# Half of the expert down-projection by three passes of high and low parts, and the shift of x in rows of 512 over three engines

## The chip, the core and the metric

One core of a Trainium2 chip runs the whole program. The metric is the device time of one execution in microseconds (us). The kernel before takes 1606.7 us (median of three runs, 1605.95 to 1608.96).

## The reference, cut to what matters

A decoder layer on 1024 tokens of width 2048, all in float32: a mixing sub-layer (spatial gating and stick-breaking attention), then a mixture of experts. Each token picks two of 32 experts. What an expert does with the rows `xb` of its tokens:

```python
def expert_block(args):
    xb, e = args
    act = jax.nn.silu(xb @ w_gate[e]) * (xb @ w_up[e])
    return act @ w_down[e]
```

`w_gate[e]` and `w_up[e]` are 2048 x 256, `w_down[e]` is 256 x 2048. The rows `xb` are normalised, scaled and shifted by a per-column vector (`* (1 + scale2) + shift2`) before the experts; the results are weighted, gated and added into the output.

## The kernel before, in words

The change lies in the last stage, which runs the 32 experts one after the other from about 945 us on. For every expert one tile of 128 token rows is gathered into `xg` (`gather_e`, L1327, issued by GpSimd, POOL), scaled, turned by TensorE (PE) in four chunks of 512 columns (`turn`, L1257), shifted, multiplied with gate and up weights (`gateup`, L1285), passed through SiLU (`act`, L1294), turned again (`turn_act`, L1300), multiplied with the down weights in four column groups of 512 (`down`, L1307), and scattered with addition into the output (`scatter_e`, L1330, POOL).

Precision is kept in two ways. Gate and up run in three passes of a faster matmul format (`float32r`): a weight tile is rounded to a high part `wh` by ScalarE (ACT, L1281), VectorE (DVE) subtracts it to get the low part `wl` (L1282), and `gateup` adds xh*wh, xh*wl and xl*wh. The shift makes `xh` and `xl` from PSUM, in four ACT and four DVE instructions of 128 columns each per chunk (L1270, L1272). The down product is one plain float32 matmul per half of the 256 rows (L1314), which the chip runs as two instructions; so a column group is four PE instructions.

The order of work is written by hand (L1398 to L1436), and every engine runs its instructions in the order in which the program issues them. The loop over experts e has eight steps q = 0 to 7. Step q multiplies two of the 16 chunks of weights (six matmuls), prepares weights three steps ahead, and interleaves what belongs to the neighbours: in the odd steps chunk q//2 of the next expert is turned ahead of `gateup` and shifted at the end of the step; the previous expert's `turn_act` comes at q = 2 and its four `down` groups at q = 3, 4, 5, 6; after the last of them, at q = 6, its scatter is issued. The gather for expert e+2 is issued at the head of loop e. Weights come in tiles of 1 MB (four for gate and up, two for down) through a ring of 12 slots, issued by SyncE (SP) in the program's order as slots come free.

Gather and scatter go in up to three pieces of rows (`pieces`, L1317). The second and third are inside `tc.If` on the expert's token count, on POOL alone: where a piece is not needed, POOL's sequencer runs instead an instruction that advances the semaphore (`INC_SWDGE_SEM`, shown at L1322).

Of the kernel before, what the change touches and what calls it, by code (L numbers as in the profile page):

```python
# [10 lines left out]
F32 = mybir.dt.float32  # L11
F32R = mybir.dt.float32r
I32 = mybir.dt.int32
AF = mybir.ActivationFunctionType
ALU = mybir.AluOpType
AX = mybir.AxisListType

P = 128
S = 1024
D = 2048  # L20
# [6 lines left out]
NE = 32  # L27
# [31 lines left out]
def body(ctx, tc, A, out):  # L59
    nc = tc.nc  # L60
    V, G, T, SC, SY = nc.vector, nc.gpsimd, nc.tensor, nc.scalar, nc.sync
    PS = bass.MemoryType.PSUM

    keep = ctx.enter_context(tc.tile_pool(name="keep", bufs=1))
# [2 lines left out]
    moe = ctx.enter_context(tc.tile_pool(name="moe", bufs=1))  # L67
    big_ = ExitStack()
    big = big_.enter_context(tc.tile_pool(name="big", bufs=2, reuse_waits="tile"))
    c1 = ExitStack()  # L70
    c1k = c1.enter_context(tc.tile_pool(name="c1k", bufs=1, reuse_waits="tile"))

# [7 lines left out]
    hcol = keep.tile([P, 10], F32, name="hcol")  # L80
    bgr = keep.tile([P, 36], F32, name="bgr")
    mhalf = keep.tile([P, 4], F32, name="mhalf")
    ident_r = keep.tile([P, P], F32R, name="ident_r")
    negm_r = keep.tile([P, P], F32R, name="negm_r")
    tri_r = keep.tile([P, P], F32R, name="tri_r")
    comp_r = keep.tile([P, P], F32R, name="comp_r")
    ccol = c1k.tile([P, 16], F32, name="ccol")
    tcst = []
    gcol = c1k.tile([P, 2, 16], F32, name="gcol")
# [356 lines left out]
    with tc.manual_schedule():  # L446
# [114 lines left out]
        for t in range(HT):  # L561
            b = (30, 33, 34, 35)[t]
# [488 lines left out]
            self.R = onehot(rt, 0, self.t)  # L1051

    def onehot(pool, b, t):
        R = []
        for i in range(2):
            R.append(pool.tile([P, P], F32, name="R", bufs=4 if b else 2))
            V.tensor_scalar(R[i], iota, float(b * P), rank[i][:, t:t + 1], op0=ALU.add, op1=ALU.is_equal)
        return R

# [133 lines left out]
    def pool(name, bufs=1):  # L1193
        return ctx.enter_context(tc.tile_pool(name=name, bufs=bufs, reuse_waits="tile"))
# [3 lines left out]
    ypools = [pool("ypool")]  # L1198
    wpa = pool("wpa", 4)
    wpb = pool("wpb", 4)  # L1200
    xpool = pool("xpool", 6)
    wpe = pool("wpe")
    wpr = pool("wpr")
    lpool = pool("lpool", 4)
    mw = pool("mw", 3)
    sl = pool("sl")
    xg = [pool("xg0").tile([P, D], F32, name="xg0")]
    wpc = pool("wpc", 2)
    hpool = pool("hpool", 4)
    xg.append(pool("xg1").tile([P, D], F32, name="xg1"))  # L1210
    wpools = [wpa] * 4 + [wpc] * 2 + [wpr] + [wpb] * 4 + [wpe]
    nw = [0]

    def wtile(shape):
        nw[0] += 1
        return wpools[(nw[0] - 1) % len(wpools)].tile(shape, F32, name="wx")
# [11 lines left out]
    class Expert:  # L1228
# [13 lines left out]

        def load_out(self):
            self.wd = []
            for f in range(2):
                w = wtile([P, D])
                SY.dma_start(w, self.wd_[f * P:(f + 1) * P, :])
                self.wd.append(w)

        def scale(self, b, on_act=True):  # L1250
# [13 lines left out]
                c = b * 4 + j  # L1264
                T.transpose(self.p[:, j, :], self.x[:, c * P:(c + 1) * P], ident)  # L1265

        def shift(self, b):
            xh, xl = self.xh[b], self.xl[b]
            for j in range(4):
                SC.activation(xh[:, j, :], self.p[:, j, :], AF.Identity, bias=b2c[:, b * 4 + j:b * 4 + j + 1])  # L1270
            for j in range(4):
                V.scalar_tensor_tensor(xl[:, j, :], self.p[:, j, :], b2c[:, b * 4 + j:b * 4 + j + 1],  # L1272
                                       xh[:, j, :].bitcast(F32), op0=ALU.add, op1=ALU.subtract)
# [26 lines left out]
        def turn_act(self):  # L1300
            p = pt2.tile([P, 4, P], F32, name="tp")
            for f in range(2):
                T.transpose(p[:, f, :], self.a[:, f * P:(f + 1) * P], ident)
            self.aT = mw.tile([P, 2, P], F32, name="actT")
            SC.activation(self.aT, p[:, 0:2, :], AF.Copy)  # L1305

        def down(self, cg):  # L1307
            if cg == 0:
                ypools.append(ypools.pop(0))
                self.y = ypools[0].tile([P, D], F32, name="y2")  # L1310
            cs = slice(cg * 512, (cg + 1) * 512)
            d = pd2.tile([P, 512], F32, name="dn")
            for f in range(2):
                T.matmul(d, self.aT[:, f, :], self.wd[f][:, cs], start=(f == 0), stop=(f == 1))  # L1314
            V.tensor_tensor(self.y[:, cs], d, gate2[:, cs], op=ALU.mult)  # L1315

    def pieces(e, move):  # L1317
# [12 lines left out]
    def scatter_e(e, y):  # L1330
        pieces(order[e], lambda r, ix: scatter(y[r], ix))

    cregs = {}
    if True:
# [56 lines left out]
            ex[0].scale(b, b % 2 == 0)  # L1391
        for b in range(3):
            ex[0].turn(b)
            ex[0].shift(b)
        V.tensor_scalar(mx[:, 1:8], iota[0:1, FIRST + 1:FIRST + 8], float(P), mx[:, 0:1], op0=ALU.mult, op1=ALU.is_lt)
        V.tensor_reduce(mx[:, 0:1], mx[:, 1:8], axis=AX.X, op=ALU.add)
        V.tensor_copy(nblk, mx[:, 0:1])
        for e in range(NE):  # L1398
            x, nx, px = ex[e], ex[e + 1] if e + 1 < NE else None, ex[e - 1] if e else None
            if nx and e:  # L1400
                nx.load_in()
            if e:
                x.load_out()
            if 0 < e < NE - 2:
                begin(e + 2)
            at_q = (2, 3, 4, 5, 6) if nx else (3, 5, 6, 7, 8)
            for q in range(8):
                if nx and q % 2 and (e, q) != (0, 1):
                    nx.turn(q // 2)
                x.gateup(q)  # L1410
                if e == 0 and q == 1:
                    x.turn(3)
                    x.shift(3)
                    begin(2)
                    nx.scale(0)
                if px and q == at_q[0]:
                    px.turn_act()
                if px and q in at_q[1:]:
                    px.down(at_q.index(q) - 1)
                    if q == at_q[4]:  # L1420
                        scatter_e(e - 1, px.y)
                if q < 5:
                    x.split(q + 3)
                elif nx:
                    nx.split(q - 5)
                if q % 2 == 0:
                    if q < 6 and nx:
                        nx.scale(q // 2 + 1)
                    elif q == 6 and e + 2 < NE:
                        ex[e + 2].scale(0)  # L1430
                if q == 7:
                    x.act()
                if (e, q) == (0, 1):
                    nx.turn(0)
                if nx and q % 2:
                    nx.shift(q // 2)  # L1436
        px.down(3)
        scatter_e(NE - 2, px.y)
        x.turn_act()
        for cg in range(4):  # L1440
            x.down(cg)
        scatter_e(NE - 1, x.y)

    ms.close()
# [4 lines left out]
    with tc.If(nmore > 0):  # L1449
        val = wtile([P, NT, 2, 3, NE])  # L1450
        for t in range(NT):
            for i in range(2):
                E, c = sl.tile([P, NE], F32, name="E", bufs=2), slice(t, t + 1)
                V.tensor_scalar(E, iom, ex_col[i][:, c], None, op0=ALU.is_equal)
                for a, f in enumerate((tok[:, c], wt_col[:, t, i:i + 1], rs_col[:, c])):
                    V.tensor_scalar(val[:, t, i, a, :], E, f, None, op0=ALU.mult)
        for b in range(1, NT):
            pt_ = pd2.tile([P, 512], F32, name="dn")
            table_start(pt_)
            for t in range(NT):  # L1460
                place(pt_, onehot(sl, b, t), [val[:, t, i] for i in range(2)], t == NT - 1)
            tb = sl.tile([P, NE, 3], I32, name="tb")
            V.tensor_copy(tb[:, :, 0], pt_[:, 0:NE])
            for i in (1, 2):
                V.tensor_copy(tb[:, :, i].bitcast(F32), pt_[:, i * NE:(i + 1) * NE])
            G.dma_start(tab_d[(b - 1) * NE:b * NE].rearrange("e p w -> p e w"), tb)
        with tc.For_i(0, nmore, 1) as b:
            with tc.For_i(0, NE, 1) as e:
                tb = mw.tile([P, 3], I32, name="tb2", bufs=2)
                SY.dma_start(tb, tab_d[ds(b * NE + e, 1)].rearrange("o p w -> (o p) w"))  # L1470
                V.memset(xg[0], 0.0)
                x = Expert(A["w_gu"][ds(e, 1)].rearrange("o q p k g f -> (o q) p k g f"),
                           A["w_down"][ds(e, 1)].rearrange("o d f -> (o d) f"),
                           xg[0], tb[:, 1:2].bitcast(F32), tb[:, 2:3].bitcast(F32))
                x.load()
                gather(xg[0], tb[:, 0:1])
                for c in range(4):
                    x.scale(c)
                    x.turn(c)
                    x.shift(c)  # L1480
                for q in range(8):
                    x.split(q)
                    x.gateup(q)
                x.act()
                x.turn_act()
                for c in range(4):
                    x.down(c)
                scatter(x.y, tb[:, 0:1])

# [33 lines left out]
```

## Time and profile before

| | |
|---|---|
| median of three runs | 1606.7 us |
| the profiled execution | 1609.03 us |
| its span, first to last instruction | 1607.2 us |
| mean granted clock of PE | 0.976 |
| instructions | 21345 |

The span is what the views below cut up. Times in the views are microseconds from its start, unless they are marked ns or stand as the mean of one instruction, which is in ns. "Busy" is time in which an engine executes; PE is the matmuls, PEld the loading of PE's weights ahead of them. In a timeline row the first number is the start, the second the duration, and a bracket gives the idle time of that engine before it and what the profile names as the releaser. The profile lists matmuls with overlapping ends, so the pace of PE is read from starts.

### The profile page before, as it was taken

Reading aid. Unit: us, or ns where it says so; the run is one execution under the profiler, and the core shown is the slowest. Engines: PE = TensorE matmul, PEld = TensorE weight load, DVE = VectorE, ACT = ScalarE, POOL = GpSimd, SP = SyncE. Lnnn points to the kernel's source line nnn. Section 1 sums busy time; section 2 is a strip of 40 time slices with the busy share of each in tenths; the row PEclk is TensorE's granted clock in tenths of the full one; section 3 lists DMA queues with packets and bytes.
Section 4 is the critical chain, followed back from the end, with each engine's and each line's share of the span. In section 5 each row is a group of like instructions: output and inputs, shape, how many; then the busy total and the mean of one; then the engine's idle time right before and its main releaser. Section 6 shows DMA issues by size and latency. Waiting matters only on the chain.

```text
span 1607.2 us, 21345 instructions
## 1 busy us (share of the span) xinstructions
PE 1516.0 (94%) x6818; PEld 1150.1 (72%) x6818; DVE 1216.5 (76%) x2220; ACT 949.0 (59%) x2016; POOL 309.7 (19%) x286
## 2 busy tenths in 40 slices
PE   4999998999999888899999969999999999999996
PEld 4788886788888665578878856666666666666663
DVE  5889675867787588768865768888888888888783
ACT  4442587754435577532222468777777777777771
POOL 2000132010011244310001211223222112223121
PEclk8899999999999999999999969999999999999998
DMA  9987477778876000368866648999999999999992
GB/s 378 353 317 245 153 258 287 238 246 298 301 272 228 9 1 1 114 225 281 295 211 264 234 167 317 364 362 374 362 383 359 355 361 361 350 375 345 377 331 43
DMA packets 94393, 433.94 MB, mean 270 GB/s; under 512 B 13072, under 2 KB 13184, under 8 KB 64192
## 3 DMA queue, kind: packets, MB, share of 16 engines
q1 hardware_dynamic: 82000, 377.54, 63.3%
q0 software_dynamic: 11984, 52.85, 11.3%
q10 hardware_dynamic: 288, 2.10, 0.3%
q8 instruction: 56, 0.92, 0.2%
q14 instruction: 65, 0.53, 0.1%
HBM read 399.89 MB, written 43.02 MB: 276 GB/s over the span
## 4 chain that ended last, share of the span: by engine, by line
PE 69%; DMA 12%; DVE 5%; ACT 5%; issue 5%; POOL 2%; SPq 0%; POOLq 0%; ACTq 0%; DVEq 0%; another core or an unknown queue 0%
PE acc L322 22%; PE gu L1291 16%; PE dn L1314 10%; PE acc L867 9%; DMA out<-y,idx 4%; DMA xg<-u_d,idx 3%; PE tp L1265 3%; DMA wm<-in_w_mod 2%; DMA out<-xi 2%; PE lg L913 1%; PE yp L719 1%; POOL sl L683 1%; PE z L655 1%; DVE macc L182 1%; DVE sp L681 1%
## 5 line engine op out<-in xcount | busy, mean ns | idle before, releaser
L1282 DVE TENSOR_TENSOR wl<-wx,wh 128x1024 fp32r<-128x1024 f32 x256 | 309.3, 1218 | 14.7 <-ACT wh L1281 13.7
L1281 ACT ACTIVATE wh<-wx 128x1024 fp32r<-128x1024 f32 x256 | 273.5, 1070 | 34.0 <-PE gu L1291 33.5
L1314 PE MATMUL dn<-wx,actT 128*128 128x512 f32 x512 | 240.1, 592 | 0.6 <-ACT actT L1305 0.5
L1291 PE MATMUL gu<-wh,xh 128*128 128x512 f32 x512 | 239.0, 467 | 0.0
L182 DVE SCALAR_TENSOR_TENSOR macc<-wm,sc_c,macc 128x512 f32<-128x512 f32 x296 | 222.2, 751 | 12.0 <-DMA wm<-in_w_mod 3.9
L322 PE MATMUL acc<-wh,hh 128*128 128x512 f32 x640 | 209.6, 398 | 3.8 <-ACT hh L278 1.8
L322 PE MATMUL acc<-wl,hh 128*128 128x512 f32 x640 | 206.6, 393 | 2.8 <-DVE wl L307 2.6
L322 PE MATMUL acc<-wh,hl 128*128 128x512 f32 x640 | 205.4, 391 | 0.3 <-DVE hl L279 0.3
L1291 PE MATMUL gu<-wl,xh 128*128 128x512 f32 x512 | 202.6, 396 | 0.1
L1291 PE MATMUL gu<-wh,xl 128*128 128x512 f32 x512 | 201.6, 394 | 0.0
L1224 POOL DMA_INDIRECT out<-y,idx x52 | 94.4, 1816 | 438.9 <-DVE y L1315 432.8
L867 PE MATMUL acc<-wo,yh 128*128 128x512 f32 x512 | 170.2, 414 | 0.0
L1315 DVE TENSOR_TENSOR y<-dn,gate 128x512 f32<-128x512 f32 x128 | 88.5, 691 | 103.2 <-PE dn L1314 103.2
L1270 ACT ACTIVATE xh<-tp,b2c 128x128 fp32r<-128x128 f32 x512 | 146.9, 383 | 19.8 <-PE tp L1265 19.8
L1314 PEld LDWEIGHTS dn<-wx,actT 128*128 128x128 f32 x512 | 96.1, 188 | 75.4 <-issue 63.2
L1272 DVE SCALAR_TENSOR_TENSOR xl<-tp,b2c,xh 128x128 fp32r<-128x128 f32 x512 | 143.4, 343 | 4.1 <-ACT xh L1270 4.1
L322 PEld LDWEIGHTS acc<-wl,hh 128*128 128x128 f32 x640 | 120.8, 189 | 29.9 <-DVE wl L307 5.0
L322 PEld LDWEIGHTS acc<-wh,hl 128*128 128x128 f32 x640 | 120.7, 189 | 26.6 <-DVE hl L279 1.0
L322 PEld LDWEIGHTS acc<-wh,hh 128*128 128x128 f32 x640 | 119.2, 189 | 27.9 <-ACT hh L278 1.9
L307 DVE TENSOR_TENSOR wl<-w,wh 128x1024 fp32r<-128x1024 f32 x80 | 97.5, 1220 | 33.5 <-ACT wh L306 33.4
L306 ACT ACTIVATE wh<-w 128x1024 fp32r<-128x1024 f32 x80 | 83.0, 1053 | 64.2 <-PE acc L322 54.2
L1291 PEld LDWEIGHTS gu<-wl,xh 128*128 128x128 f32 x512 | 97.2, 190 | 30.3 <-issue 14.8
(246 smaller groups left out, 2316.3 us busy)
## 6 DMA issues: line engine op xcount, KB each, us to landing
wx<-in_w_gu SPq DMA_DIRECT2D x128, 1024.0 KB, 22.5
wm<-in_w_mod SPq DMA_DIRECT2D x160, 512.0 KB, 5.3
wx<-in_w_down SPq DMA_DIRECT2D x64, 1024.0 KB, 21.6
w<-in_w_in SPq DMA_DIRECT2D x80, 512.0 KB, 5.4
x<-in_w_mod SPq DMA_DIRECT2D x16, 1024.0 KB, 6.1
wo<-in_w_out SPq DMA_DIRECT2D x16, 512.0 KB, 4.8
xi<-in_x SPq DMA_DIRECT2D x24, 256.0 KB, 5.9
out<-xi SPq DMA_DIRECT2D x24, 256.0 KB, 3.9
```

The costliest lines, as they stand in the source:

```text
L182: V.scalar_tensor_tensor(self.acc, t[:, j, :], sc, self.acc, op0=ALU.mult, op1=ALU.add)
L307: V.tensor_tensor(wl, w, wh.bitcast(F32), op=ALU.subtract)
L322: T.matmul(accs[t], a, b, start=(first and j == 0 and n == 0), stop=(last and j == 1 and n == 2))
L867: T.matmul(acc, y[a][:, c, ts_], w[b][:, c % 2, :], start=(n_ == 0 and i == 0), stop=(n_ == 7 and i == 2))
L1224: return G.indirect_dma_start(out=out, out_offset=bass.IndirectOffsetOnAxis(ap=idx, axis=0), in_=y, in_offset=None, bounds_check=S - 1, oo ...
L1270: SC.activation(xh[:, j, :], self.p[:, j, :], AF.Identity, bias=b2c[:, b * 4 + j:b * 4 + j + 1])
L1272: V.scalar_tensor_tensor(xl[:, j, :], self.p[:, j, :], b2c[:, b * 4 + j:b * 4 + j + 1], xh[:, j, :].bitcast(F32), op0=ALU.add, op1=ALU.sub ...
L1281: SC.activation(self.wh[q], w, AF.Copy)
L1282: low = lambda: V.tensor_tensor(self.wl[q], w, self.wh[q].bitcast(F32), op=ALU.subtract)
L1291: T.matmul(self.gu, a[c // 4][:, c % 4, :], b[q][:, k, :], start=(c == 0 and i == 0), stop=(c == 15 and i == 2))
L1314: T.matmul(d, self.aT[:, f, :], self.wd[f][:, cs], start=(f == 0), stop=(f == 1))
L1315: V.tensor_tensor(self.y[:, cs], d, gate2[:, cs], op=ALU.mult)
```

## The change

Two of the four column groups of `down` (1 and 3) are computed as three `float32r` passes. ACT rounds the group's weights to `dh`, DVE makes the low part `dl` (`split_down`), and `turn_act` makes `ah` (ACT) and `al` (POOL) beside `actT`. The down weights are stored and loaded in two halves of columns instead of two halves of rows, so that a half is free once its two groups are done. `shift` becomes one DVE addition over 512 columns from PSUM into a new single-buffered tile `xf`; its rounding (ACT) and subtraction (POOL) are returned as a function, which the loop calls in the following step (`later`). The first expert's chunks keep the old form. Buffers shrink or move to make room: `xpool` 6 to 5, `mw` 3 to 1, four constants to a pool that is closed before the experts.

```diff
     def onehot(pool, b, t):
-        R = []
+        if b:
+            both = pool.tile([P, 4, P], F32, name="xf")
+            R = [both[:, i, :] for i in range(2)]
+        else:
+            R = [pool.tile([P, P], F32, name="R", bufs=2) for _ in range(2)]
...
-    xpool = pool("xpool", 6)
+    xpool = pool("xpool", 5)
...
-    mw = pool("mw", 3)
+    mw = pool("mw")
     sl = pool("sl")
...
+    dpool = pool("dpool")
...
         def load_out(self):
             self.wd = []
-            for f in range(2):
-                w = wtile([P, D])
-                SY.dma_start(w, self.wd_[f * P:(f + 1) * P, :])
+            for h in range(2):
+                w = wtile([P, 2, D // 2])
+                SY.dma_start(w, self.wd_[h])
                 self.wd.append(w)
...
-        def shift(self, b):
+        def shift(self, b, fast=False):
             xh, xl = self.xh[b], self.xl[b]
+            if not fast:
+                x = sl.tile([P, 4, P], F32, name="xf")
+                V.tensor_tensor(x, self.p, b2c[:, b * 4:b * 4 + 4].unsqueeze(2).to_broadcast([P, 4, P]), op=ALU.add)
+
+
+                def parts():
+                    SC.activation(xh, x, AF.Copy)
+                    G.tensor_tensor(xl, x, xh.bitcast(F32), op=ALU.subtract)
+                return parts
...
             SC.activation(self.aT, p[:, 0:2, :], AF.Copy)
+            self.ah = mw.tile([P, 2, P], F32R, name="actH")
+            self.al = mw.tile([P, 2, P], F32R, name="actL")
+            SC.activation(self.ah, p[:, 0:2, :], AF.Copy)
+            G.tensor_tensor(self.al, self.aT, self.ah.bitcast(F32), op=ALU.subtract)
+
+        def wd_of(self, cg):
+            return self.wd[cg // 2][:, :, cg % 2 * 512:cg % 2 * 512 + 512]
+
+        def split_down(self, cg):
+            self.dh = dpool.tile([P, 2, 512], F32R, name="dh")
+            self.dl = dpool.tile([P, 2, 512], F32R, name="dl")
+            SC.activation(self.dh, self.wd_of(cg), AF.Copy)
+            V.tensor_tensor(self.dl, self.wd_of(cg), self.dh.bitcast(F32), op=ALU.subtract)
...
-            for f in range(2):
-                T.matmul(d, self.aT[:, f, :], self.wd[f][:, cs], start=(f == 0), stop=(f == 1))
+            if cg % 2:
+                for f in range(2):
+                    for i, (a, b) in enumerate(((self.ah, self.dh), (self.ah, self.dl), (self.al, self.dh))):
+                        T.matmul(d, a[:, f, :], b[:, f, :], start=(f == 0 and i == 0), stop=(f == 1 and i == 2))
+            else:
+                for f in range(2):
+                    T.matmul(d, self.aT[:, f, :], self.wd_of(cg)[:, f, :], start=(f == 0), stop=(f == 1))
             V.tensor_tensor(self.y[:, cs], d, gate2[:, cs], op=ALU.mult)
...
+        later = []
         for e in range(NE):
...
                 if px and q == at_q[0]:
                     px.turn_act()
+                    px.split_down(1)
                 if px and q in at_q[1:]:
                     px.down(at_q.index(q) - 1)
+                    if q == at_q[2]:
+                        px.split_down(3)
                     if q == at_q[4]:
                         scatter_e(e - 1, px.y)
...
+                if later:
+                    later.pop()()
                 if nx and q % 2:
-                    nx.shift(q // 2)
+                    later.append(nx.shift(q // 2))
         px.down(3)
         scatter_e(NE - 2, px.y)
+        x.split_down(1)
         x.turn_act()
         for cg in range(4):
             x.down(cg)
+            if cg == 1:
+                x.split_down(3)
```

## Rows read from the trace of the kernel before

**Rows 1.** The page, part 1: busy time, share and instructions of each engine.

```profile
PE 1516.0 (94%) x6818; PEld 1150.1 (72%) x6818; DVE 1216.5 (76%) x2220; ACT 949.0 (59%) x2016; POOL 309.7 (19%) x286
```

**Rows 2.** Busy time by stage; columns: stretch, us, busy time of each engine, PEclk, DMA, GB/s.

```profile
1100.00:1200.00 100.00, 99.92 (x410) 68.70 (x409) 82.81 (x145) 75.07 (x150) 27.05 (x17) 1.00 1.00 372
...
1200.00:1220.00 20.00, 20.00 (x83) 13.82 (x82) 16.57 (x29) 15.17 (x31) 3.17 (x2) 1.00 0.97 379
```

**Rows 3.** The chain of waits from 900 us on: start, us, work.

```profile
1199.48 1.72 PE dn L1314 x4
1201.20 1.39 PE gu L1291 x6
...
1219.48 1.72 PE dn L1314 x4
```

**Rows 4.** Costliest groups of instructions, and those of POOL: busy us, mean ns.

```profile
L1282 DVE TENSOR_TENSOR wl<-wx,wh 128x1024 fp32r<-128x1024 f32 x256 | 309.3, 1218 | 14.7 <-ACT wh L1281 13.7
L1281 ACT ACTIVATE wh<-wx 128x1024 fp32r<-128x1024 f32 x256 | 273.5, 1070 | 34.0 <-PE gu L1291 33.5
...
L1270 ACT ACTIVATE xh<-tp,b2c 128x128 fp32r<-128x128 f32 x512 | 146.9, 383 | 19.8 <-PE tp L1265 19.8
L1272 DVE SCALAR_TENSOR_TENSOR xl<-tp,b2c,xh 128x128 fp32r<-128x128 f32 x512 | 143.4, 343 | 4.1 <-ACT xh L1270 4.1
...
L849 DVE TENSOR_TENSOR yld<-tr,hcol 128x512 f32<-128x512 f32 x4 | 2.7, 684 | 0.0
L853 ACT ACTIVATE yh<-yld 128x512 fp32r<-128x512 f32 x4 | 2.5, 634 | 2.4 <-DVE yld L849 2.4
...
L683 POOL TENSOR_TENSOR sl<-sp,sh 128x512 fp32r<-128x512 f32 x24 | 30.7, 1279 | 41.1 <-DVE sh L682 30.8 <-PE yp L719 8.0 <-PE cum L697 2.3
L854 POOL TENSOR_TENSOR yl<-yld,yh 128x512 fp32r<-128x512 f32 x8 | 11.7, 1463 | 44.4 <-ACT yh L853 44.4
...
L683 POOL TENSOR_TENSOR sl<-sp,sh 128x256 fp32r<-128x256 f32 x8 | 5.8, 731 | 8.7 <-DVE sh L682 6.0 <-PE cum L709 2.3 <-PE yp L719 0.3
```

**Rows 5.** Timeline of DVE around the end of one expert.

```profile
1204.34 0.69 DVE L1315 TENSOR_TENSOR y<-dn,gate 128x512 f32<-128x512 f32 x1 [0.24 <-PE dn L1314]
...
1207.62 1.12 DVE L1272 SCALAR_TENSOR_TENSOR xl<-tp,b2c,xh 128x128 fp32r<-128x128 f32 x4
1208.67 1.21 DVE L1282 TENSOR_TENSOR wl<-wx,wh 128x1024 fp32r<-128x1024 f32 x1
```

**Rows 6.** Timeline of PE's weight loads: gateup of step 3, then the second down group.

```profile
1211.29 0.19 PEld L1291 LDWEIGHTS gu<-wl,xh 128*128 128x128 f32 x1
...
1215.56 0.41 PEld L1314 LDWEIGHTS dn<-wx,actT 128*128 128x128 f32 x2
```

**Rows 7.** Timeline of POOL: scatters (L1224) and the gathers (L1220) behind them.

```profile
1187.74 1.31 POOL L1224 DMA_INDIRECT out<-y,idx  x1 [0.30 <-issue]
...
1205.31 2.12 POOL L1224 DMA_INDIRECT out<-y,idx  x1 [14.57 <-DVE y L1315]
1211.16 1.05 POOL L1220 DMA_INDIRECT xg<-u_d,idx  x1 [3.73 <-ACT xh L1270]
...
1469.40 1.68 POOL L1224 DMA_INDIRECT out<-y,idx  x1 [0.30 <-issue]
```

**Rows 8.** All scatters; POOL's skips (L1322) before and after 1330 us, min/median/max ns.

```profile
L1224 POOL DMA_INDIRECT out<-y,idx x52 | 94.4, 1816 | 438.9 <-DVE y L1315 432.8
...
L1322 POOLq INC_SWDGE_SEM  x50: 1475/2302/2682, 953.3 to 1327.2; - x50
...
L1322 POOLq INC_SWDGE_SEM  x36: 377/712/1097, 1332.4 to 1596.5; - x36
```

**Rows 9.** Busy time by stage around two waits of PE; columns as in rows 2.

```profile
826.00:830.00 4.00, 1.24 (x9) 0.94 (x8) 2.84 (x5) 1.10 (x4) 0.00 (x0) 1.00 0.34 131
830.00:834.00 4.00, 4.00 (x14) 3.09 (x13) 1.23 (x1) 0.83 (x1) 0.00 (x0) 0.58 0.25 43
...
1487.00:1492.00 5.00, 4.04 (x20) 2.77 (x19) 2.57 (x6) 4.27 (x9) 2.76 (x3) 1.00 1.05 385
```

More of the change, by code (lines that the diff above doesn't have):

```diff
@@ L69, in body @@
     big = big_.enter_context(tc.tile_pool(name="big", bufs=2, reuse_waits="tile"))
+    big1 = big_.enter_context(tc.tile_pool(name="big1", bufs=1))
+    ident_r, negm_r, tri_r, comp_r = (big1.tile([P, P], F32R, name=f"cr{i}") for i in range(4))
     c1 = ExitStack()
@@ L82, in body @@
     mhalf = keep.tile([P, 4], F32, name="mhalf")
[L83 to L86, printed above, removed]
     ccol = c1k.tile([P, 16], F32, name="ccol")
@@ L1053, in onehot @@
     def onehot(pool, b, t):
-        R = []
+        if b:
[3 more added lines that the diff above has]
+            R = [pool.tile([P, P], F32, name="R", bufs=2) for _ in range(2)]
         for i in range(2):
-            R.append(pool.tile([P, P], F32, name="R", bufs=4 if b else 2))
             V.tensor_scalar(R[i], iota, float(b * P), rank[i][:, t:t + 1], op0=ALU.add, op1=ALU.is_equal)
@@ L1393, in body @@
             ex[0].turn(b)
-            ex[0].shift(b)
+            ex[0].shift(b, True)
         V.tensor_scalar(mx[:, 1:8], iota[0:1, FIRST + 1:FIRST + 8], float(P), mx[:, 0:1], op0=ALU.mult, op1=ALU.is_lt)
@@ L1412, in body @@
                     x.turn(3)
-                    x.shift(3)
+                    x.shift(3, True)
                     begin(2)
@@ L1472, in body @@
                 x = Expert(A["w_gu"][ds(e, 1)].rearrange("o q p k g f -> (o q) p k g f"),
-                           A["w_down"][ds(e, 1)].rearrange("o d f -> (o d) f"),
+                           A["w_down"][ds(e, 1)].rearrange("o h p k f -> (o h) p k f"),
                            xg[0], tb[:, 1:2].bitcast(F32), tb[:, 2:3].bitcast(F32))
@@ L1479, in body @@
                     x.turn(c)
-                    x.shift(c)
+                    x.shift(c)()
                 for q in range(8):
@@ L1486, in body @@
                 for c in range(4):
+                    if c % 2:
+                        x.split_down(c)
                     x.down(c)
@@ L1500 @@
     arr = {"x": I["x"][0], "w_mod": tiles(I["w_mod"], 2), "w_in": tiles(I["w_in"][0], 2),
-           "w_out": tiles(I["w_out"][0], 2), "w_gu": wgu, "w_down": I["w_down"][0]}
+           "w_out": tiles(I["w_out"][0], 2), "w_gu": wgu,
+           "w_down": I["w_down"][0].reshape(NE, 2, P, 2, D // 2).transpose(0, 3, 2, 1, 4)}
     arr["consts"] = const_blob()
```

## The prediction, made before the changed kernel was run

> **What bounds the kernel now.** I read the page first: PE is busy for 94% of the span, far ahead of DVE and ACT [rows 1]. An average says nothing of a stage, so the busy time by stage comes next. In the experts, the only stage that the change touches, PE is busy for all of 100 us, DVE for 83%, ACT for 75%; in one period of 20 us DVE works 16.57, ACT 15.17 and POOL only 3.17 us [rows 2]. The chain of waits shows the beat: the same down group starts at 1199.48 and at 1219.48, so an expert takes 20.0 us, and PE hardly waits in it [rows 3]. PE's instruction stream is the bound, the DMA engines are full beside it (share 0.97 to 1.00) [rows 2], and POOL looks idle. The views to read last are therefore the timelines, for what the change makes PE wait for.
>
> **The change part by part.** *PE.* Four float32 down instructions hold PE for 1.72 us, six float32r instructions for 1.39 [rows 3]. The new groups 1 and 3 are six of the latter: 0.33 us saved each, 0.66 an expert. For 31 experts that is 20.5 us. The last expert has nothing beside its downs; there `dh` and `dl` for group 3 can only be made after group 1 (one buffer), about 1.07 + 1.21 us [rows 4, 5] against one group of 1.72, which eats its 0.66: nothing.
>
> *DVE.* Per expert it loses four groups of shift instructions, 1.12 each [rows 5], and gains four additions over 512 columns from PSUM, 0.68 each, and two `dl`, 1.22 each [rows 4]: 16.57 - 4.48 + 2.74 + 2.44 = 17.27 us [rows 2]. Against a period of 19.34 that fits, with little to spare.
>
> *ACT.* Out go four groups of four, 146.9/128 = 1.15 us each; in come four roundings of 0.63, two `dh` of 1.07 and `ah` (no row has it in this form; half of a 512-column rounding is 0.32, the whole 0.63, I take 0.4, nearer the half) [rows 4]: 15.17 - 4.60 + 2.54 + 2.14 + 0.4 = 15.65 us. `dh` of group 3 waits for PE to end group 1 and holds the weight rounding behind it; those roundings are made three steps ahead, so I cost it at nothing; without that lead each would cost up to a step, 2.5 us.
>
> *POOL.* It gains `al`, 0.73, and four subtractions over 512 columns, 1.28 each, or 1.46 by the slower row [rows 4]. In sum that is 6 us on an engine that is busy for 3. The order matters, not the sum. The tile `xf` has one buffer: DVE can't write the next chunk until POOL has subtracted the one before. The subtraction of chunk 2 is issued at step 6, *behind the scatter*, and that of chunk 3 at step 0, *behind the gather*. POOL takes its instructions in order, and DVE does too, with the low parts of gateup's weights behind its addition.
>
> **First wait: chunk 2 behind the scatter.** Count from the start of the last `y`, 1204.34 [rows 5]. The scatter starts at 0.97 and takes 2.12 [rows 7]. Gateup of step 3 loads for its `wl` at 1211.29 [rows 6], 6.95 after `y`. DVE needs 0.69 for `xf` and 1.21 for that `wl` before it, so the subtraction must be over 5.05 after `y`. By pieces of the scatter:
> - Two pieces: the second runs at 3.09 + 0.30 to 4.70 [rows 7], the subtraction from 5.0 to 6.3: 1.25 us late.
> - Three: the third adds 0.30 + 1.68 [rows 7], 8.3: 3.2 us late.
> - One: the two skipped pieces hold POOL's sequencer. They have a median of 2.30 us each in the first two thirds of the stage, 0.71 in the last third [rows 8]. The trace of before shows this as the gather starting 3.73 us after the scatter's end with nothing else for it to wait for [rows 7]. Early, the subtraction goes from 0.92 + 2 x 2.30 + 0.25 = 5.8 to 7.1: 2.0 late. Late in the stage it goes from 3.4 to 4.7: in time.
>
> The 52 scatter instructions [rows 8] are, counted in that timeline, 16 experts of one piece, 12 of two and 4 of three. Of those of one piece 14 come in loops with a later chunk to shift, 8 before 1330 us. Sum: 12 x 1.25 + 4 x 3.2 + 8 x 2.0 = 44 us. PE recovers none of it, since the next `y` comes later by the same time.
>
> **Second wait: chunk 3 behind the gather.** The new `dl` of group 1 stands on DVE behind `xf` of the next chunk 0, which waits for the subtraction of chunk 3. The group starts at 1215.56 [rows 6]; its second pass, one instruction (0.23) later, needs `dl`, 11.45 after `y`. Early in the stage, with one piece each: gather and two more skips follow the first subtraction's issue by 1.5 us and take 2 x 2.3 + 0.2, so chunk 3 is subtracted from 12.1 to 13.4, `xf` and `dl` end at 15.3: 3.9 late in all, 1.9 more than the first wait. By the same steps, with each pair's own pieces and skips, four pairs of one piece give 8.3 more, four with a gather of three pieces 8.6, the rest 4.6: 21.5 us. Its lower bound is nothing, if the first wait has set PE back far enough.
>
> **The sum.** 44 + 21.5 - 20.5 = 45 us slower. The profiled execution took 1609.03 us, 2.3 above the median; 1654 on its scale is 1652 on that of the median.
>
> **Edits at nothing.** The two loads of down weights have the same count and size; the first half's slot comes free two groups earlier. With `xpool` at 5 a chunk's buffer is that of the chunk before it in the current expert, whose gateup ended two steps earlier. With `mw` at 1, `act` and `actT` are read out steps before they are written again. The moved constants and the second form of `onehot` run no instruction in this stage. If one of these covers were gone, a wait of a step, 2.5 us an expert, would appear at `xh` or `actT`.
>
> **The rivals.**
> - *Faster: POOL keeps up.* Decided by the subtraction of chunk 2: if it ends within 5.05 us of `y` in nearly all experts, PE gains 20.5. For it: late in the stage the one-piece experts do so. Against: 16 of 30 scatters have more pieces, whose time is in rows. Then the weights become the limit, since DMA is full already: 1586 if they follow, 1597 if half is lost.
> - *No change: the weights hold the pace.* PE's gain and POOL's waits both disappear in a stage paced by DMA at 20 us an expert: 1605 to 1609. DMA moves 372 to 379 GB/s in these stretches [rows 2] and PE still never waits. The Trainium skill's page "DMA: Bandwidth & Descriptors", section Specifications, states a limit of about 358 GB/s of HBM for a core; by it, loads couldn't come faster and no gain would be left. The trace is above that figure, so the measurement decides.
> - *Slower by less.* Only part of the first wait shows, because skips are short once other work stands between them: 12 x 1.25 + 4 x 3.2 - 20.5 = 7 us, 1610 to 1630, with 1614 by the sum.
> - *Slower by more: the clock falls too.* After a wait of some 2.8 us in a stretch, PE ran at 0.58 of its clock (mostly the lower level, 1.2 GHz) for the next 4 us; after one near 1 us it stayed at 1.00 [rows 9]. Some 15 of the waits above are over 2 us. At half clock 4 us of work lose 2, and half as much again for a second stretch: 15 x 2 to 3 = 30 to 45 us, 1682 to 1697. The Trainium skill's "TensorE: Matmul & The Clock Gate", section HAM oscillation, warns that gaps between bursts of matmuls bring the throttle back each time; here the next wait can swallow it, since PE at half speed arrives later.
>
> **How the numbers follow.** POOL's two waits 0.52 (1630 to 1680), clock as well 0.10, slower by less 0.12, no change 0.05, faster 0.21. About 0.2% is what a measurement of this kernel can tell from none. Faster 0.21, same 0.05, slower 0.74. The likeliest case gives 1652; its own range is 1630 (no second wait) to 1680 (subtractions at 1.46 instead of 1.28 add 0.18 to each of some 26 waits, 5 us, and a half of the lower clock's price adds the rest). Eight in ten need part of the faster case: 1596 to 1690.
>
> **What would show it.** Right: DVE idle before `xf`, released by POOL, some 45 to 65 us in all; PE idle before gateup's `wl` at step 3 and before `dl`; periods of 21 to 24 us for experts with several pieces or early in the stage, and of 19.3 for one-piece experts at the end; six down instructions in 1.39 us. DMA share falls below 0.95. Wrong: PE without gaps at 19.3 us a period (the faster case), or PE waiting for weights (`wh` on DMA), or a down group of six that takes more than 1.5 us.

## The result and the profile after

The changed kernel takes 1731.45 us (median of four runs, 1727.49 to 1733.95) against 1607.83 for the kernel before (four runs): 1.076 times its time, 95% interval 1.0738 to 1.0782. The forecast was 1652. The sign was right; the loss, 124 us, is nearly three times the 45 forecast. The profiled execution took 1733.12 us, its span is 1731.0, the mean granted clock 0.954 (0.976 before).

The page of the kernel after, part 1, answers to [rows 1]. POOL is the engine that grew, from 310 to 534 us:

```profile
PE 1555.3 (90%) x6946; PEld 1195.1 (69%) x6946; DVE 1297.3 (75%) x1912; ACT 956.8 (55%) x1740; POOL 534.0 (31%) x442
```

Busy time by stage of the kernel after, columns as in [rows 2]. The last row runs from the first product of expert 0 (`act` on DVE) to that of expert 31, so it is 31 periods:

```profile
1100.00:1200.00 100.00, 86.57 (x349) 60.99 (x348) 78.42 (x77) 62.77 (x87) 53.14 (x37) 0.96 0.90 304
1200.00:1220.00 20.00, 18.41 (x76) 13.04 (x74) 15.99 (x16) 11.89 (x16) 9.33 (x8) 0.95 1.01 354
...
977.60:1706.40 728.80, 652.08 (x2631) 463.82 (x2632) 584.23 (x583) 467.33 (x640) 366.80 (x249) 0.95 0.87 296
```

PE was busy for all of 100 us in [rows 2]; now it is for 86.6, and its clock is 0.96. The same 31 periods took 618.3 us before (967.0 to 1585.3, PE busy 616.5, clock 1.00) and take 728.8 now: 110.5 of the 124 us lie there. A period is 23.5 us, and by its busy time no engine is full.

The waits of the kernel after, 950 to 1731 us, show who holds whom (us in total, times, longest):

```profile
ACT xh L1277 <- DVE xf L1273: 206.5, 92, 5.0
...
DVE xf L1273 <- POOL xl L1278: 122.0, 48, 4.4
...
PE tp L1267 <- DVE xf L1273: 59.2, 27, 3.7
...
PEld gu L1302 <- DVE wl L1293: 37.5, 75, 1.1
```

The costliest groups that answer to [rows 4], from the page of the kernel after:

```profile
L1293 DVE TENSOR_TENSOR wl<-wx,wh 128x1024 fp32r<-128x1024 f32 x256 | 378.6, 1489 | 18.2 <-ACT wh L1292 18.2
L1278 POOL TENSOR_TENSOR xl<-xf,xh 128x512 fp32r<-128x512 f32 x124 | 205.5, 1657 | 223.6 <-ACT xh L1277 169.3
...
L1273 DVE TENSOR_TENSOR xf<-tp,b2c 128x512 f32<-128x512 f32 x124 | 84.8, 684 | 124.1 <-POOL xl L1278 122.0
```

`wl` is the same instruction as before and takes 1489 ns where it took 1218. POOL's subtraction takes 1657, more than either row of [rows 4] (1279 and 1463). Both engines became slower while they worked at the same time; `e7` and `e12` below try that alone.

One wait in full, as the timelines of POOL, DVE and PE of the kernel after show it (start, duration, idle before and releaser):

```profile
1214.25 2.15 POOL L1226 DMA_INDIRECT out<-y,idx  x1 [4.30 <-DVE y L1344]
1216.70 1.34 POOL L1226 DMA_INDIRECT out<-y,idx  x1 [0.30 <-PE gu L1302]
1218.35 1.32 POOL L1226 DMA_INDIRECT out<-y,idx  x1 [0.30 <-issue]
1219.24 1.72 POOL L1278 TENSOR_TENSOR xl<-xf,xh 128x512 fp32r<-128x512 f32 x1
```

```profile
1220.99 0.69 DVE L1273 TENSOR_TENSOR xf<-tp,b2c 128x512 f32<-128x512 f32 x1 [4.35 <-POOL xl L1278]
```

```profile
1218.03 0.38 PE L1314 MATMUL tp<-cst,act 128*128 128x128 f32 x2
1221.83 0.63 PE L1267 MATMUL tp<-cst,xg 128*128 128x128 f32 x4 [3.42 <-DVE xf L1273]
...
1223.46 0.63 PE L1302 MATMUL gu<-wh,xl 128*128 128x512 f32 x1
1223.88 0.63 PE L1302 MATMUL gu<-wh,xh 128*128 128x512 f32 x1
...
1227.41 0.39 PE L1302 MATMUL gu<-wl,xh 128*128 128x512 f32 x1
1227.64 0.39 PE L1302 MATMUL gu<-wh,xl 128*128 128x512 f32 x1
```

This is the forecast's first wait with three pieces: the subtraction of chunk 2 stands behind the scatter, DVE waits 4.35 us, PE 3.42 (forecast 3.2). Two things come with it. PE then issues a matmul each 0.42 us instead of each 0.23, that is at about the lower of its two clock levels (1.2 of 2.4 GHz; the granted clock is 0.72 from 1221 to 1224 us and 0.78 from 1224 to 1228), and is back at 0.23 by 1227.41. And PE stops at the *turn* at the head of step 3, not at the `wl` behind it: the turn needs a PSUM buffer that `xf` has not yet read.

### The profile page after: what moved, and what is told of

It reads as the page before. It is cut to its first block, busy times and chain, and to the rows that moved or that the text cites. A ratio compares the mean times of both kernels' runs of the same rounds, so it can differ in the third digit from the quotient of the medians.

```text
span 1731.0 us, 21406 instructions
## 1 busy us (share of the span) xinstructions
PE 1555.3 (90%) x6946; PEld 1195.1 (69%) x6946; DVE 1297.3 (75%) x1912; ACT 956.8 (55%) x1740; POOL 534.0 (31%) x442
## 5 line engine op out<-in xcount | busy, mean ns | idle before, releaser
L1293 DVE TENSOR_TENSOR wl<-wx,wh 128x1024 fp32r<-128x1024 f32 x256 | 378.6, 1489 | 18.2 <-ACT wh L1292 18.2
L1278 POOL TENSOR_TENSOR xl<-xf,xh 128x512 fp32r<-128x512 f32 x124 | 205.5, 1657 | 223.6 <-ACT xh L1277 169.3
L1292 ACT ACTIVATE wh<-wx 128x1024 fp32r<-128x1024 f32 x256 | 264.4, 1047 | 0.0
L1302 PE MATMUL gu<-wl,xh 128*128 128x512 f32 x512 | 218.3, 426 | 11.3 <-DVE wl L1293 8.7
L1277 ACT ACTIVATE xh<-xf 128x512 fp32r<-128x512 f32 x124 | 78.0, 629 | 207.5 <-DVE xf L1273 206.5
L1273 DVE TENSOR_TENSOR xf<-tp,b2c 128x512 f32<-128x512 f32 x124 | 84.8, 684 | 124.1 <-POOL xl L1278 122.0
L1302 PEld LDWEIGHTS gu<-wl,xh 128*128 128x128 f32 x512 | 100.3, 196 | 67.1 <-DVE wl L1293 37.5
L1267 PE MATMUL tp<-cst,xg 128*128 128x128 f32 x512 | 81.4, 284 | 71.4 <-DVE xf L1273 59.2
L126 POOL TENSOR_TENSOR rs<-rs,mhalf 128x4 f32<-128x4 f32 (+1 forms) x44 | 47.9, 1094 | 314.7 <-DVE rs L123 314.7
L1343 PE MATMUL dn<-wx,actT 128*128 128x512 f32 x256 | 129.4, 630 | 1.1 <-ACT actT L1316 1.1
L1267 PEld LDWEIGHTS tp<-cst,xg 128*128 128x128 f32 x512 | 64.1, 146 | 90.3 <-issue 64.8
```

Source lines behind the costliest of these rows:

```text
L1273: V.tensor_tensor(x, self.p, b2c[:, b * 4:b * 4 + 4].unsqueeze(2).to_broadcast([P, 4, P]), op=ALU.add)
L1277: SC.activation(xh, x, AF.Copy)
L1278: G.tensor_tensor(xl, x, xh.bitcast(F32), op=ALU.subtract)
L1292: SC.activation(self.wh[q], w, AF.Copy)
L1293: low = lambda: V.tensor_tensor(self.wl[q], w, self.wh[q].bitcast(F32), op=ALU.subtract)
L1302: T.matmul(self.gu, a[c // 4][:, c % 4, :], b[q][:, k, :], start=(c == 0 and i == 0), stop=(c == 15 and i == 2))
```

## Experiments

Each run was timed beside the kernel before on the same chip; that stood at 1609 to 1610 us in all of them, and the ratio is to it, with its 95% interval. "Waits" are those of 1000 to 1600 us. The sum of 31 periods, first to last `act`, is given as "experts" (618.3 before, 728.8 after).

**The parts alone.** `e6` has neither part, only the new memory layout (`actT` takes the room of `ah` and `al`); `e3` the new down groups; `e4` the new shift.

```diff
e6, e3:
-        def shift(self, b, fast=False):
+        def shift(self, b, fast=True):
...
-                    later.append(nx.shift(q // 2))
+                    nx.shift(q // 2)
e6, e4:
-            if cg % 2:
+            if False:
...
-            self.ah = mw.tile([P, 2, P], F32R, name="actH")
-            self.al = mw.tile([P, 2, P], F32R, name="actL")
...
-                    px.split_down(1)
```

> Both parts of the change undone (four rows of ACT and four of DVE for a shift, four float32 down groups), its memory layout and the down loads in halves kept. Theory layout: the first clear of xg0 waits as in the changed kernel (first product of expert 0 around 974 to 977 us, where before has 967), the 31 expert periods stay at 618, and the time is 1613 to 1619 us. Rival (the late start comes from the new shift or the new down groups): the start is back at 967 and the time within 2 us of before, 1606 to 1610.

> The changed kernel with the old shift (four ACT and four DVE instructions from PSUM) for all chunks; the three-pass down groups stay, and POOL has only al to subtract. Both theories: no waits for xf; 20.5 us off the experts, some 7 us lost at the start of the stage: 1590 to 1600. A rival C (the down split alone makes DVE the bound, 19.0 us of work an expert beside waits for PE): 1610 to 1630.

> The changed kernel with all four down groups in float32, no dh, dl, ah, al; the new shift stays. Theory A: the waits for xf stay, PE loses its 20.5 us: 1700 to 1740. Theory B: POOL's subtractions still slow DVE, but DVE has 2.4 us less to do an expert: below 1650. Rival C: below 1620.

Measured: `e6` 1612.9 us, 1.0027 (1.0008 to 1.0047), experts 618.5. `e3` 1612.2, 1.0024 (1.0009 to 1.0039), experts 613.1. `e4` 1661.1, 1.0332 (1.0302 to 1.0363), experts 662.0.

`e6` came out at the lower edge of its first theory. `e3` missed its 1590 to 1600: the experts gain 5.2 us, not 20.5, and PE's matmuls wait 11.7 us for POOL's `al`; its rival C (1610 to 1630) has the time but not the reason, since DVE is busy for 557.8 of 600 us. `e4` lies between its theories A and B.

So the layout costs 4 us, all before the experts. The issue of the first eight weight tiles and the first clear of `xg0` show where, in the kernel before and in `e6`:

```profile
861.69 27.09 SPq L1240 DMA_DIRECT2D wx<-in_w_gu  x8
...
922.64 1.90 ACT L1344 ACTIVATE xg<-pcol 128x2048 f32<-128x2048 f32 x1
```

```profile
861.45 59.88 SPq L1242 DMA_DIRECT2D wx<-in_w_gu  x8
...
929.18 1.91 ACT L1369 ACTIVATE xg<-pcol 128x2048 f32<-128x2048 f32 x1 [6.68 <-DMA wx<-in_w_gu]
```

In `e6` tiles stand on memory that earlier work gives back later; the clear waits 6.68 us and the first product comes at 973.9 instead of 967.0.

The two parts alone cost 2 and 51 us, each with the layout's 4 in it, and together 124. The waits of `e4` say why they don't add:

```profile
1000.00:1600.00 600.00, 569.69 (x2284) 386.43 (x2283) 436.99 (x475) 367.14 (x502) 310.82 (x202) 0.99 0.96 342
```

```profile
DVE xf L1273 <- POOL xl L1278: 117.5, 46, 4.5
...
PE tp L1267 <- DVE xf L1273: 26.1, 22, 3.0
```

DVE waits for POOL about as long as in the full change, but its work and its waits fill 437 + 117.5 = 554.5 of 600 us. The rest is slack in which DVE catches up, and only 26 us reach PE at the turn. In the full change DVE has `dl` as well: 584.2 + 122.0 = 706 of 728.8 us, next to no slack, and 59 us reach PE.

**Off POOL.** `e8` gives both of POOL's subtractions to DVE, `e10` only `al`.

```diff
-                    G.tensor_tensor(xl, x, xh.bitcast(F32), op=ALU.subtract)
+                    V.tensor_tensor(xl, x, xh.bitcast(F32), op=ALU.subtract)
...
-            G.tensor_tensor(self.al, self.aT, self.ah.bitcast(F32), op=ALU.subtract)
+            V.tensor_tensor(self.al, self.aT, self.ah.bitcast(F32), op=ALU.subtract)
```

> The changed kernel with both of POOL's subtractions (xl from xf and xh, al from actT and actH) on DVE: POOL has its transfers alone again. Theory contention and order alike: wl back at 1.22 to 1.25, DVE xf waits for POOL no more. By DVE's work (17.3 us an expert before; four rows of 684 and four of 634 for sixteen of 383, two of 1211 for dl, some 0.4 for al) about 19 us an expert, so the experts take 600 to 630 us and the time is 1600 to 1640. Rival: DVE waits for ACT's rounding in each step (as xh now stands behind wh in ACT's order), a new chain between ACT and DVE, periods of 22 or more and a time over 1680.

> The changed kernel with al alone moved from POOL to DVE; xl stays on POOL. The two parts alone took about 3 us (new down groups) and 52 us (new shift) over before and together 124. Theory two queues meet: al stands in POOL's order between xl and the transfers and holds both, so without it the sum is that of the parts, 1655 to 1685. Rival (DVE's two more rows of 1.21 an expert under POOL's load are what is too much): over 1710, as DVE has still more to do.

Measured: `e8` 1608.9 us, 0.9997 (0.9977 to 1.0017), experts 614.6. `e10` 1743.3, 1.0808 (1.0779 to 1.0837). `e8` came out as expected: it takes the whole loss back by moving 156 instructions to an engine that was *busier*: the rest of the change is worth some 4 us in the experts, about what the layout costs. `e10` was a miss: `al` was not what joined the parts. Over the 31 periods DVE works 601.5 us in it (584.2 in the kernel after), and the periods are 16 us longer.

**Which chunks.** Only chunks 2 and 3 stand behind a scatter or a gather. `e14` leaves chunks 0 and 1 on POOL, `e15` chunks 2 and 3, the same amount of POOL work.

```diff
-                    G.tensor_tensor(xl, x, xh.bitcast(F32), op=ALU.subtract)
e14:
+                    (V if b > 1 else G).tensor_tensor(xl, x, xh.bitcast(F32), op=ALU.subtract)
e15:
+                    (V if b < 2 else G).tensor_tensor(xl, x, xh.bitcast(F32), op=ALU.subtract)
```

> The changed kernel with xl of chunks 2 and 3 (the ones that stood behind the scatter and the gather) on DVE; chunks 0 and 1 and al stay on POOL. Theory order: what the prediction charged is gone, no wait of DVE xf for POOL over 2 us, half of the contention stays: 1625 to 1665. Rival (the wait comes at every chunk, from POOL's and DVE's slow rows): about half way between e8 and the changed kernel, 1665 to 1690, and within 15 us of e15.

> The changed kernel with xl of chunks 0 and 1 on DVE; chunks 2 and 3, which stand behind the scatter and the gather, stay on POOL with al. Theory order: the waits stay, DVE xf waits for POOL 90 us or more in the stage, 1690 to 1735. Rival (every chunk alike): 1665 to 1690.

Measured: `e14` 1625.1 us, 1.0104 (1.0076 to 1.0131), experts 624.2. `e15` 1706.0, 1.0589 (1.0563 to 1.0615), experts 706.0. The waits of `e14`, then of `e15` with its busy time:

```profile
DVE xf L1273 <- POOL xl L1278: 17.6, 9, 3.4
```

```profile
DVE xf L1273 <- POOL xl L1278: 111.4, 42, 4.8
...
PE tp L1267 <- DVE xf L1273: 51.7, 23, 4.0
```

```profile
1000.00:1600.00 600.00, 543.00 (x2219) 392.45 (x2220) 475.11 (x545) 397.30 (x546) 219.24 (x163) 0.95 0.92 318
```

The place decides: 97 us over `e8` with the two chunks behind the transfers, 16 with the other two. Slower rows of DVE are not the reason: `wl` takes 1261 ns in `e15` and 1370 in `e14`. Both times lie in the range of the order theory; only `e14`'s longest wait, 3.4 us, is over the 2 us that it allowed. `e15` also has nearly all of the lost clock (0.95), `e14` hardly any (0.99). This is the forecast's mechanism, order on POOL, shown by itself.

**Ahead of the transfers.** `e1` calls the rounding and the subtraction at the head of the next step or loop, before the scatter and before the gather.

```diff
+            if later:
+                later.pop()()
             if 0 < e < NE - 2:
                 begin(e + 2)
...
+                if later and q % 2 == 0:
+                    later.pop()()
                 if px and q == at_q[0]:
```

> The changed kernel with ACT's rounding and POOL's subtraction issued earlier: those of chunk 2 ahead of the scatter at step 6, those of chunk 3 ahead of the gather at the head of the loop, the others at the start of their step. The same instructions in another order. Theory A (POOL's order and the one xf buffer make DVE wait): DVE's waits for POOL before xf fall from 122 us to under 20, the lower clock goes with PE's long waits, and the experts take what the undisturbed ones of the changed kernel take, about 20.5 us instead of 23.5: 31 x 3 = 93 us less, about 1640. Theory B (POOL's subtractions slow DVE's two-input instructions, so that DVE is the bound, wherever they stand): the time stays above 1700.

Measured: 1770.2 us, 1.1006 (1.0975 to 1.1038), worse than the change itself. DVE never waits for POOL any more. Instead, the waits show ACT:

```profile
ACT xh L1277 <- DVE xf L1273: 234.6, 97, 3.9
DVE dl L1329 <- ACT dh L1328: 77.0, 48, 2.2
DVE wl L1293 <- ACT wh L1292: 65.2, 51, 1.6
```

The rounding moved with the subtraction. At the head of the step it waits for an addition that DVE has not reached, and holds ACT's weight roundings behind it, for which DVE then waits. Neither theory had that: theory B's time (above 1700) came, but not its reason, since DVE is busy for 451.9 of 600 us. A wait moved from one in-order queue to another.

**Two buffers.** `e2` gives `xf` two buffers (and `xpool` four, for room); `e11` has that and `al` on DVE.

```diff
-                x = sl.tile([P, 4, P], F32, name="xf")
+                x = sl.tile([P, 4, P], F32, name="xf", bufs=2)
...
-    xpool = pool("xpool", 5)
+    xpool = pool("xpool", 4)
```

> The changed kernel with two xf buffers (and xh, xl with four instead of five to make room); the order stays. Theory A: DVE no longer waits for POOL, the low parts themselves are needed some 3 us later than they come; about 1640, as with the other order. Theory B: above 1700, since POOL's work and DVE's are the same.

> As e10, with two buffers of xf (and xpool 4). Theory waits: with nobody held by POOL's order, only DVE's slower rows are left, 1615 to 1645. Rival (the wait of PE for xl itself, as the rounding and POOL's row follow one another a step late): PE waits for POOL's xl and the time stays over 1660.

Measured: `e2` 1683.5 us, 1.0473 (1.0441 to 1.0505), between the two expectations. DVE's wait falls to 14.4 us, but PE's matmuls wait 40.7 us for `al`, which is in POOL's order too. `e11` 1653.6, 1.0255 (1.0229 to 1.0282), a little above what was expected: nobody is held long by POOL's order, the clock is 0.99, and 43 us of loss remain. `e10` and `e11` differ by the second buffer (and `xpool`) alone: it takes away 90 us. The 43 that remain I read as what both engines lose side by side, since `wl` takes 1574 ns there; the next pair tries that alone.

**POOL and DVE side by side.** `e7` is `e6`, that is neither part of the change, with a subtraction on POOL for each shift whose result nobody reads; `e12` is the same beside `e8` (with `xpool` 4 and `waste` in another pool, for room).

```diff
+            waste = dpool.tile([P, 4, P], F32R, name="waste")
+            G.tensor_tensor(waste, gate2[:, 0:512].rearrange("p (j n) -> p j n", n=P), xh.bitcast(F32), op=ALU.subtract)
```

> The kernel of e6 with one subtraction of 128x512 on POOL for each shift, from xh and gate2 into a tile that nobody reads (124 of them), so that POOL works as in the changed kernel and nothing waits for it. Theory contention: wl on DVE (1.22 us in before) rises to 1.35 to 1.55 as a mean, DVE becomes full, the periods rise by 1 to 2.5 us and the time is 1640 to 1695. Rival order (POOL's work costs only where somebody waits for it): wl stays under 1.27 and the time is within 4 us of e6.

> e8 (all subtractions on DVE) with a subtraction of 128x512 on POOL for each shift that nobody waits for (and xpool 4 for room). In e7, where DVE had 1.9 us an expert to spare, the same load cost 6 us. Here DVE is busy 569 of 600. Theory contention with a full DVE: wl 1.22 to about 1.47, 234 rows x 0.25 = 58 us more in 600, of which 31 fit: 1635 to 1670. Rival (POOL's load costs next to nothing by itself): under 1620.

Measured: `e7` 1619.1 us, 1.0064 (1.0043 to 1.0084), 6 us over `e6`; `e12` 1718.0, 1.0659 (1.0633 to 1.0685), 109 us over `e8`. The groups of `e8`, then of `e12`, 1000 to 1600 us:

```profile
L1293 DVE TENSOR_TENSOR wl<-wx,wh 128x1024 fp32r<-128x1024 f32 x233 | 284.9, 1223 | 1.5 <-ACT wh L1292 1.3 <-DMA wx<-in_w_gu 0.3
...
L1344 DVE TENSOR_TENSOR y<-dn,gate 128x512 f32<-128x512 f32 x123 | 84.5, 687 | 5.2 <-PE dn L1340 3.6 <-PE dn L1343 1.5
...
L1278 DVE TENSOR_TENSOR xl<-xf,xh 128x512 fp32r<-128x512 f32 x115 | 79.5, 691 | 13.0 <-ACT xh L1277 13.0
```

```profile
L1295 DVE TENSOR_TENSOR wl<-wx,wh 128x1024 fp32r<-128x1024 f32 x204 | 319.3, 1565 | 0.1
...
L1278 DVE TENSOR_TENSOR xl<-xf,xh 128x512 fp32r<-128x512 f32 x102 | 82.4, 808 | 0.0
...
L1346 DVE TENSOR_TENSOR y<-dn,gate 128x512 f32<-128x512 f32 x102 | 69.0, 677 | 0.0
```

The instructions with two operands in SBUF grow (`wl` 1223 to 1565, `xl` 691 to 808); those that read PSUM do not (`y` 687 to 677). One of them beside POOL's, from the timelines of `e12`:

```profile
1203.60 1.21 DVE L1331 TENSOR_TENSOR dl<-wx,dh 128x1024 fp32r<-128x1024 f32 x1
1204.73 2.32 DVE L1295 TENSOR_TENSOR wl<-wx,wh 128x1024 fp32r<-128x1024 f32 x1
1206.97 0.68 DVE L1278 TENSOR_TENSOR xl<-xf,xh 128x512 fp32r<-128x512 f32 x1
```

```profile
1203.94 2.02 POOL L1280 TENSOR_TENSOR waste<-gate,xh 128x512 fp32r<-128x512 f32 x1 [6.02 <-ACT xh L1277]
```

POOL's row ends at 1203.94 + 2.02 = 1205.96; with the 1.21 us of an undisturbed `wl` that makes 1207.17, close to the 1207.05 at which this one ends: DVE's instruction stands until POOL's is over and then takes about its usual time. It is so all through the stage of `e12`: the 70 `wl` of over 1.4 us all end 1.08 to 1.09 us after a row of POOL, and none without such a row beside it takes over 1.23. The Trainium skill's "SBUF — State Buffer", section SBUF: two separate sides, says that a GpSimd instruction that reads SBUF and a VectorE instruction with two inputs in SBUF exclude one another for a whole instruction; these rows agree.

What it costs depends on DVE's slack. In `e7` `wl` rises nearly as much, to 1470, and DVE has room: 539.3 of 600 us. (The expectation had `wl` right and the time wrong, since it took DVE to be full there.) In `e12` it has none, and since it never stands still, no wait can be the cause:

```profile
1000.00:1600.00 600.00, 534.80 (x2187) 368.80 (x2188) 599.88 (x612) 391.37 (x536) 317.19 (x187) 0.99 0.92 312
```

The expectation for `e12` was too low by nearly 50 us: it added `wl`'s growth alone, but `dl` (1220 to 1402), `xl` and `al` (417 to 979) grow too.

**Repaired.** `e9` is `e3` with `al` on DVE and `dh` and `dl` placed ahead of `xf` and `xg0`; `e13` is `e8` with the same placement.

```diff
+    dpool = pool("dpool")
     sl = pool("sl")
...
-    dpool = pool("dpool")
```

> The new down groups alone, with the old shift, al on DVE in place of POOL, and the tiles dh and dl put in front of xf and xg0 in memory, so that xg0 and what follows stand where they stand in before. If the layout made the late start by xg0's place: start back at 967, experts 605 to 613, time 1594 to 1604, faster than before. If the start hangs on other tiles (the first weight tiles, 2 KB lower): start still 974, time 1602 to 1612. If DVE is full and al in its order costs more than POOL's wait did: periods over 20 and time over 1615.

> e8 with dh and dl in front of xf and xg0 in memory, as in e9. The first clear of xg0 no longer waits, first product of expert 0 some 6 us earlier after the loads' start: 1600 to 1605, as e9, faster than before. If e8's later experts already made up for the late start: 1606 to 1610.

Measured: `e9` 1602.2 us, 0.9947 (0.9930 to 0.9965), experts 609.3; `e13` 1601.3, 0.9934 (0.9910 to 0.9959), experts 612.6. Both came out as expected. In both the first clear of `xg0` no longer waits. Both beat both kernels; between them there is no difference that these runs can tell.

## Why the prediction was wrong in size and right in sign

The forecast added up PE's time. Its sum against the trace, for the span (1731.0 - 1607.2 = 123.8 us):

| term | forecast | measured |
|---|---|---|
| PE's saving | -20.5 | -15.5 (PE busy over the experts: 601.0 in `e8`, 616.5 before) |
| PE idle, both waits | +65.5 | +74.9 (728.8 - 652.1 = 76.7, against 1.8) |
| PE at the lower clock | a rival | +32 to 34 (68.3 us at the lower level, PE busy in 63.7 of them; half is lost) |
| PE's rows longer for other reasons | not in it | +17 to 19 (what is left of 652.1 - 601.0) |
| start later | 0 | +10.6 (977.6 against 967.0) |
| end longer | 0 | +2.7 |

This says where PE's time went, not what set the pace. DVE's time shows that, between the same two products (us; one profile each):

| kernel | 31 periods | DVE works | it waits for POOL's `xl` | it waits for PE |
|---|---|---|---|---|
| after | 728.8 | 584.2 | 122.0 | 5.0 |
| `e15` | 706.0 | 562.0 | 124.6 | 2.5 |
| `e10` | 745.2 | 601.5 | 124.4 | 2.8 |
| `e4` | 662.0 | 482.4 | 121.8 | 38.7 |

The kernel after's waits of DVE in that stretch, but for the 122.0 and 0.8 us for `dh`:

```profile
DVE wl L1293 <- ACT wh L1292: 16.2, 31, 0.8
DVE xf L1273 <- PE dn L1343: 2.1, 1, 2.1
DVE y L1344 <- PE dn L1340: 1.9, 2, 1.7
DVE y L1344 <- PE dn L1343: 1.0, 2, 0.8
```

*The step that failed: DVE's 17.27 us of work were held against a period of 19.34 ("that fits, with little to spare") without the time for which DVE stands and waits, and PE stayed the bound.* In the kernel after DVE works 584.2 / 31 = 18.85 us an expert, waits 122.0 / 31 = 3.94 for POOL and 0.52 for ACT's `wh`: 23.3 of the 23.5 us. It hardly waits for PE. So DVE and POOL, each in its own order, set the period, and PE's gaps are what is left over. `e15` and `e10` have the same waits with less and more work on DVE, and the periods follow it nearly one for one: 22 us less work, 23 us less time; 17 more, 16 more. In `e4` DVE waits for POOL as long, but has 102 us less to do; there it waits for PE too, and the loss stays at 51 us. The prediction put DVE's waits at 45 to 65 us and priced only what came too late for PE.

*Why DVE's work was too small: its 17.27 and POOL's 6 us an expert were added up as if apart.* POOL's subtraction took 1657 ns, above the upper price of 1.46, and `wl` 1489. Only POOL's row was given a range, and DVE's was held at [rows 4], whose `wl` ran with POOL nearly idle. The term is small where DVE has slack (`e7`: 6 us) and nearly as large as the whole loss where it has none (`e12`: 109).

*The two waits.* Right in place: `e14` and `e15` show that the chunks behind scatter and gather carry nearly all. In size they were mixed. PE's idle time at the turn of step 3 is 59.2 us (forecast 44, at the `wl` behind it), before `dl` it is 6.4 (forecast 21.5). Three pieces are near the forecast (3.42 for 3.2); two pieces take mostly 1.9 to 2.1 us for 1.25, and early scatters of one piece 1.95 to 3.7 for 2.0. Late experts of one piece each way run at 19.8 to 21.9 us, not 19.3.

*The clock* was a rival with one chance in ten, at 30 to 45 us. For PE's own time that price was right: the trace has 17 stretches at the lower level, 12 of the 13 gaps of PE of 2 us or more have one at their end, and 5 of the 9 of 1.5 to 2 us. But no run shows that it cost the kernel time. In two periods of the kernel after, with two pieces of scatter and two of gather each, the clock stays up in the first and falls in the second:

```profile
1143.83:1167.26 23.43, 20.85 (x87) 14.42 (x86) 19.01 (x21) 15.38 (x23) 13.41 (x10) 1.00 0.96 338
1192.72:1216.16 23.44, 21.25 (x86) 15.12 (x85) 19.02 (x20) 15.25 (x23) 12.32 (x10) 0.93 1.00 338
```

Both take 23.4 us; the same two experts of `e15` take 22.46 at 1.00 and 22.43 at 0.92. So the prediction's remark that the next wait can swallow the lost time is borne out, as PE is the one that waits. It also makes it in part luck that PE's idle time came out near the forecast: at the full clock PE would have stood longer, by up to 34 us (an estimate from the 68.3 us).

*PE.* Right by the row: the six instructions of a new group take 1.40 us by their starts, a plain group 1.71 (forecast 1.39 and 1.72). Over 62 groups that is 19.2 us; why PE's busy time fell by 15.5 (`e8`) and 16.3 (`e3`) only stays open. The 17 to 19 us of longer rows I read as short waits of PE's weight loads for `wl` (37.5 us in the list above). `e15` has about half of both (13.9 against 29.0 us of these waits from 1000 to 1600 us, and 9 of longer rows), but it was not tried by itself.

*Edits at nothing.* The memory layout was not nothing: `e6` shows 4 us in the time and 7 at the start of the stage, `e9` and `e13` get them back (from the first weight load's issue to the first product it is 105 to 106 us in them and before, 112 in `e6`). Of the other 3 to 4 of the 10.6, 2.6 stand ahead of that issue, and single profiles differ there by as much (858.7 to 864.3 us). The tail, where `dh` and `dl` were costed at nothing, is 2.7 longer.

*The rivals.* "Faster" named its condition rightly: with POOL's subtractions off the path the change is even, and with the layout repaired it is 0.7% faster, less than the 1586 to 1597 forecast, since DVE is then busy 569 of 600 us (`e8`). The weights were never the limit: GB/s fell to 296.

## What to carry to other kernels

Before work goes to an engine because it looks idle, read where in that engine's *order* it will stand and who waits for it there: two of four subtractions on POOL cost 97 us in one place and 16 in another. Add to each engine's work the time for which it will stand and wait before you say that it fits: DVE's 17.3 us in a period of 19.3 left no room for waits of 3.9. Work on POOL is not beside DVE's when both read two operands in SBUF, as here; price it in DVE's slack. And before a lower clock of PE gets a price, ask whether PE sets the pace: here periods with it and without it took the same time.

## What was not expected of the hardware

That DVE's rows grow by the whole remaining time of POOL's instruction, and by operands: `wl`, `dl`, `xl` and `al` grow in `e12`, `xf` and `y`, which read PSUM, stay within 2%. And that a scratch subtraction that nobody waits for costs 109 us in one kernel and 6 in another, at nearly the same length of its own (1753 and 1674 ns).
